# Attention logits of two query blocks at a time: one whole-array pass each, and two half-array passes in two row groups of TensorE

## The chip, the cores and the metric

The kernel runs on one core of one Trainium2 chip. The metric is the device time of one execution in microseconds (us), the median over several runs. Five engines of the core matter here: TensorE (PE in the profile; PEld is its weight loads, which have a row of their own), VectorE (DVE), ScalarE (ACT), GpSimd (POOL), and SyncE (SP), whose queue issues nearly all DMA transfers.

## The reference

The program is one layer of a decoder block: a mixer in which eight heads of forgetting attention stand beside a gated unit with spatial mixing, and then a gated feed-forward part with a short convolution. The sequence has 1024 positions, the model 1024 channels, and all is float32. The part that is changed is the logits of the attention, for each head `h` and each block of 128 queries:

```python
logits = jnp.einsum('bqhd,bkhd->bhqk', qi, k).astype(jnp.float32) * scale   # Dh = 64
logits = logits + ci[..., None] - c_k          # c = cumsum(log_sigmoid(forget))
logits = jnp.where(causal, logits, -jnp.inf)
p = jax.nn.softmax(logits, axis=-1).astype(v.dtype)
return jnp.einsum('bqhk,bkhd->bqhd', p, v)
```

A head has 64 channels, 1024 keys and 8 blocks of queries. Block `j` needs keys 0 to 128(j+1) only.

## The kernel before, in words

**Numbers in two parts.** TensorE is fed float32 values in a rounded format (`F32R`), one pass for each product. To keep float32 precision each operand is split into a high part (rounded) and a low part (what the rounding left), and a product is made of several passes. Elsewhere three passes are made: high by high, high by low, low by high.

**Logits before.** A head has only 64 channels, and a pass contracts over 128 rows of the array. So the high part of the queries is put in rows 0 to 63 and the low part in rows 64 to 127 of one tile `A`. The tile `B` has the keys in the same way (high over low), `B2` has them turned over (low over high). One pass of `A` with `B` gives high by high plus low by low; one with `B2` gives high by low plus low by high. Each logits tile of 128 queries by up to 512 keys (a "piece", `(j, c)`, `c` the first key) is these two passes, at L1007 and L1008, into one of three PSUM banks (`lbank`). There are 12 pieces in a head, 96 in all: in a head, 6 are 512 keys wide, and two each 128, 256 and 384.

**Around it.** `Head` holds a head's tiles; `head_loads` fetches `A`, `B`, `B2` and the row `ck` of forget sums from DRAM scratch (`qd`, `kd`, `ncd`, written by the projection stage before). `select` masks the forget row on GpSimd, `least` (L1015) adds it to the logits on VectorE while it finds the row minimum, `expo` makes the exponentials on ScalarE, `turn` (L1028) transposes them on TensorE, `cast` and `lows` split them, and `weigh` (L1047) multiplies them with the values. `Gated` gives the same loop a filling of other TensorE work: the output projection of the gated unit (`fl`, L1123). A loop of 96 steps runs over heads and groups; before the change each step takes one piece from `stream`, and 10 pieces are made before the loop.

**What sets the order.** Everything up to the end of attention is written down in that loop and then ordered again by a planner in the kernel (`Pace`): `settle` collects the instructions with their dependences and a table of costs (`cost`), `run` simulates the engines and picks for each engine the ready instruction with the earliest due time. The order of each engine, SP's transfers included, is fixed to what it picks. What comes after `settle` (output projection of the attention at L1364 to L1366, then the feed-forward part) is not planned by it.

**Scratch tiles.** Tag `raw` is a ring of four 512 KB tiles for weights as they come from DRAM; during attention it holds the weights of the gated unit's output (`wos`) and then those of the attention's (`woa`, four of them, all loaded at step 54).

Of the kernel before, what the change touches and what calls it, by code (L numbers as in the profile page):

```python
# [14 lines left out]
P = 128  # L15
# [17 lines left out]
class Pace:  # L33
# [1 line left out]


    def __init__(self, tc):
        self.tc, self.slot, self.ring, self.prev, self.held = tc, {}, {}, {}, {}

    def keep(self, t, key):  # L40

# [108 lines left out]
    def settle(self, rounds=3):  # L150

        names = {mybir.EngineType.PE: "PE", mybir.EngineType.DVE: "DVE", mybir.EngineType.Activation: "ACT",
                 mybir.EngineType.Pool: "POOL", mybir.EngineType.SP: "SP"}
        ops, seen, uses, opens = [], {}, {}, {}
        for i in list(self.tc.nc.cur_bb.bb.instructions)[self.first:]:
            eng = names.get(i.engine)
            rd = [v for v in map(self.view, i.ins) if v]
            wr = [v for v in map(self.view, i.outs) if v]
            if eng is None or not wr:
                continue  # L160
            k = len(ops)
            if eng == "PE" and not i.start_tensor_calc:
                rd = rd + wr
            deps = set()
            for w, vs in ((False, rd), (True, wr)):
                for name, a, b, m, tile_ in vs:
                    old, keep, hits = seen.setdefault(name, []), [], 0
                    for o in old:
                        hit = o[2] < b and a < o[3] and o[4] & m
                        if hit and (w or o[1]):  # L170
                            deps.add(o[0])
                            hits += 1
                        if not (w and hit and a <= o[2] and o[3] <= b and not o[4] & ~m and tile_):
                            keep.append(o)
                    keep.append((k, w, a, b, m))
                    seen[name] = keep
                    if tile_:
                        uses.setdefault(name, set()).add(k)
                        if not hits:
                            opens.setdefault(name, set()).add(k)  # L180
            deps.discard(k)
            c = self.cost(i, eng)
            ops.append((i, eng, c, deps, SET.get(str(getattr(i, "func", "")).split(".")[-1], 0) if eng == "ACT" else 0))
        for name, ks in opens.items():
            old = self.prev[name]
# [4 lines left out]
        n = len(ops)  # L190
        succ = [[] for _ in range(n)]
        for k, o in enumerate(ops):
            for d in o[3]:
                succ[d].append(k)
        line, count = [k for k in range(n) if not ops[k][3]], [len(o[3]) for o in ops]
        for k in line:
            for q in succ[k]:
                count[q] -= 1
                if not count[q]:
                    line.append(q)  # L200
        assert len(line) == n, [(ops[k][0].name, str(ops[k][0])) for k in range(n) if count[k]][:4]
        at, t = [0.0] * n, 0.0
        for k, o in enumerate(ops):
            at[k] = t
            if o[1] == "PE":
                t += o[2][0]
        best = None
        for _ in range(rounds):
            due = [0.0] * n
            for k in reversed(line):  # L210
                o = ops[k]
                d = at[k] if o[1] == "PE" else at[k] + SLACK
                for s in succ[k]:
                    d = min(d, due[s] - o[2][1] - HOP)
                due[k] = d
            order, start, end = self.run(ops, succ, due)
            if best is None or end < best[0]:
                best = (end, order)
            at = start
        for eng, seq in best[1].items():  # L220
            for x, y in zip(seq, seq[1:]):
                self.tc.add_manual_dep(ops[y][0], ops[x][0].name, mybir.DependencyInfo(
                    mybir.DependencyClass.NoSync, mybir.DependencyReason.DATA), reason="order")
        return best[0]

    def run(self, ops, succ, due):
# [6 lines left out]
        port = {"DVE": 0.0, "POOL": 0.0}  # L233
        order = {e: [] for e in can}
        start = [0.0] * n
        bus, table, done, end = 0.0, 0, 0, 0.0
        for k in range(n):
            if not left[k]:
                can[ops[k][1]].append(k)
        while done < n:  # L240
            pick = None
            for e, ks in can.items():
# [5 lines left out]
                s = max(f, ready[k])  # L248
                if pick is None or s < pick[0]:
                    pick = (s, k)  # L250
            s, k = pick
            i, e, (cad, lat, x), deps, fn = ops[k]
            can[e].remove(k)
            if fn and fn != table:
# [36 lines left out]
def block_kernel(ctx: ExitStack, tc: tile.TileContext, xT, xtok, wuv, wv, wqk, wf, cpk, bfv,  # L291
# [50 lines left out]
    def f32(ap):  # L342
        return ap.bitcast(F32)
# [466 lines left out]
    def head_loads(h):  # L810
        ab, nb = sb("x1", [P, 2, 1024], F32R), sb("x2", [P, 2, 1024], F32R)
        A, B, ck, B2 = ab[:, 0, :], ab[:, 1, :], f32(nb[:, 0, :]), nb[:, 1, :]
        sp.dma_start(out=f32(A), in_=qd[h].rearrange("s d t -> (s d) t"))
        sp.dma_start(out=f32(B), in_=kd[h].rearrange("s d t -> (s d) t"))
        sp.dma_start(out=f32(B2[0:64, :]), in_=kd[h, 1])
        sp.dma_start(out=f32(B2[64:128, :]), in_=kd[h, 0])
        sp.dma_start(out=ck, in_=ncd[h:h + 1, :].to_broadcast((P, 1024)))
        return A, B, ck, B2

# [156 lines left out]
    attT = [None] * 4  # L976
    attF = [None] * 4
    TTAG = [("gg", "gg"), ("wy", "wy"), ("G0", "G2"), ("G1", "G3")]
    PIECES = [(j, c) for j in range(8) for c in range(0, (j + 1) * P, 512)]
    GROUPS = [(0, k) for k in range(4)] + [(1, k) for k in range(8)]  # L980

    class Head:

        def __init__(self, h):
            self.h, self.p, self.hh = h, h // 2, h % 2
            self.A, self.B, self.ck, self.B2 = loaded.pop(h, None) or head_loads(h)
            self.rs = sml.tile([P, 8], F32, tag="rs", name=nm("rs"))
            self.pair, self.t, self.lg, self.pt, self.po, self.mn = {}, {}, {}, {}, {}, {}

# [11 lines left out]
        def logits(self, j, c):  # L1001

            n = (j + 1) * P
            e = min(n, c + 512)
            qs = slice(j * P, (j + 1) * P)
            ps = self.lg[j, c] = lbank()
            pe.matmul(ps[:, 0:e - c], self.A[:, qs], self.B[:, c:e], start=True, stop=False)  # L1007
            pe.matmul(ps[:, 0:e - c], self.A[:, qs], self.B2[:, c:e], start=False, stop=True)  # L1008

        def least(self, j, c):  # L1010

# [60 lines left out]
    def pair_end(p, eng):  # L1072
# [3 lines left out]
        for o in (slice(0, 512), slice(512, 1024)):  # L1076
# [4 lines left out]
            eng.tensor_tensor(out=attT[p][:, 1, o], in0=f[:, 0, o], in1=f32(attT[p][:, 0, o]), op=ALU.subtract)  # L1081
            yield

    class Gated:


# [3 lines left out]
            self.place = sb("t01", [P, 2, 512])  # L1090

        def load_w(self, hf, kp):
            self.raw[hf, kp] = sb("raw", [P, 2, 512])
            sp.dma_start(out=self.raw[hf, kp], in_=wos[hf, kp])

        def split(self, hf, k):
# [40 lines left out]
    wo, wraw = [], []  # L1137

    def wo_load():
        for k in range(4):  # L1140
            wraw.append(sb("raw", [P, 1024]))
            sp.dma_start(out=wraw[k], in_=woa[k])

    def wo_split(k, hf, lo_eng):
        if hf == 0:
# [5 lines left out]
        w = wo[k][hf]  # L1151
        split_w(wraw[k][:, hf * 512:hf * 512 + 512], (w[:, 0], w[:, 1]), "act", lo_eng)

    STEPS, FILL_RATE = 96, 2.13
    heads = [Head(0)]
    exps, lates, stream = [], [], [(h, j, c) for h in range(8) for j, c in PIECES]
    FIRST = [PIECES[n] for n in (0, 1, 4, 5, 2, 3, 6, 7, 8, 9, 10, 11)]
    stream = [(0, j, c) for j, c in FIRST] + stream[12:]
    picks, nsel = [], [0]
    for h, j, c in stream:  # L1160
        if (h, j) not in picks:
            picks.append((h, j))

    def w1(k):
        return tsplit(wvr[k][:, 1, :])
# [8 lines left out]
    def piece():  # L1174

        if not stream:
            return
        h, j, c = stream.pop(0)
        if (j, c) == (0, 0) and 0 < h < 7:
            heads.append(Head(h + 1))  # L1180
        while nsel[0] < len(picks) and nsel[0] <= picks.index((h, j)) + 1 and picks[nsel[0]][0] < len(heads):
            heads[picks[nsel[0]][0]].select(picks[nsel[0]][1])
            nsel[0] += 1
        heads[h].logits(j, c)
        lates.append((h, j, c))

    def finish_piece():
        for h, j, c in lates:
# [11 lines left out]
    for i in range(8):  # L1200
# [5 lines left out]
        if 1 <= i <= 4:  # L1206
            spatial_out(2 * i - 2)
            spatial_out(2 * i - 1)
            w1s.append(w1(i - 1))
        if i in (0, 2):  # L1210
            evac_v(i, vds[i // 2][:, 0, :])
            evac_v(i + 1, vds[i // 2][:, 1, :])
        if i == 4:
# [1 line left out]
                gated.load_w(0, kp)  # L1215
            gated.load_x((0, 0))
            heads.append(Head(1))
        for _ in range((0, 0, 1, 1, 1, 2, 2, 2)[i]):
            piece()
            finish_piece()  # L1220
        if i >= 4:
# [13 lines left out]
    for s in range(STEPS + BEHIND + 1):  # L1235
# [15 lines left out]
        run_exps()  # L1251
        if s < STEPS:
            heads[h].lows(*GROUPS[g])
        piece()
        finish_piece()
        if g == 2 and h < 8:
            heads[h].sums_a()
        for m in {0: (0, 1, 2), 1: (3,)}.get(s, ()):
# [534 lines left out]
```

## Time and profile before

| | |
|---|---|
| median of 3 runs | 1074.86 us (1074.78 to 1076.51) |
| profiled execution: time / span of the records | 1075.99 us / 1074.3 us |
| TensorE matmul busy | 1053.2 us, 98% of the span, 4885 matmuls |
| weight loads busy | 865.8 us |
| VectorE, ScalarE, GpSimd busy | 905.7, 574.8, 238.9 us |
| first to last logits pass | 208.8 to 364.5 us |

Busy time of TensorE is not the same as work at its peak: matmuls overlap (a pass of 512 columns is shown with 389 ns, while passes in a row start 227 ns apart), so the start-to-start distance is what a pass costs. A DMA's time to landing is counted from its issue. The profile is of one execution.

### The profile page before, as it was taken

The numbers are of one execution on the slowest core, as the hardware profiler recorded it, in microseconds if no ns is written. First come the engines' busy times: TensorE is split into PE (matmuls) and PEld (weight loads), VectorE is DVE, ScalarE is ACT, GpSimd is POOL, SyncE is SP. The second block draws the span as 40 slices with busy tenths as digits, with TensorE's granted clock in tenths as the row PEclk, the third lists the DMA queues.
The fourth block names the chain that finished last, engine by engine and source line by source line (L and its number), as shares of the span: only waits on it lengthen the run. The fifth ranks groups of instructions, "written<-read, shape, count | busy, mean of one in ns | idle before, by whom it ended". The sixth has DMA issues, their size and how long they took to land.

```text
span 1074.3 us, 14284 instructions
## 1 busy us (share of the span) xinstructions
PE 1053.2 (98%) x4885; PEld 865.8 (81%) x4885; DVE 905.7 (84%) x1390; ACT 574.8 (54%) x1006; POOL 238.9 (22%) x211
## 2 busy tenths in 40 slices
PE   9999999999999999998999999999999999999997
PEld 6888778788888877876888888888888888888886
DVE  6986699898888868999899899998998776898774
ACT  6657445577776746753444444444344444454653
POOL 0002224232362250054233232233322000000000
PEclk9999999999999999999999999999999999999999
DMA  9243336886675354223323323232331998333442
GB/s 333 96 145 98 90 115 176 265 255 189 193 220 158 109 199 164 77 73 125 120 67 119 126 82 115 99 114 83 108 118 50 302 342 305 106 92 99 144 122 96
DMA packets 64712, 158.16 MB, mean 147 GB/s; under 512 B 7672, under 2 KB 7936, under 8 KB 64640
## 3 DMA queue, kind: packets, MB, share of 16 engines
q1 hardware_dynamic: 64352, 156.70, 44.8%
q8 instruction: 38, 0.62, 0.2%
q10 hardware_dynamic: 288, 0.56, 0.1%
q14 instruction: 34, 0.28, 0.1%
HBM read 114.95 MB, written 42.27 MB: 146 GB/s over the span
## 4 chain that ended last, share of the span: by engine, by line
PE 82%; issue 7%; DVE 5%; DMA 3%; POOL 2%; ACT 1%; SPq 0%; POOLq 0%; DVEq 0%; ACTq 0%
PE s L1455 20%; PE b L1455 14%; PE s L1650 11%; PE b L1650 8%; PE s L493 6%; PE b L493 5%; PE fl L1123 4%; PE po L1047 3%; PE tr L1028 3%; PE b L635 2%; PE s L635 2%; PE lg L1008 2%; PE lg L1007 2%; DMA qd<-G 1%; DMA x<-kd 1%
## 5 line engine op out<-in xcount | busy, mean ns | idle before, releaser
L1455 PE MATMUL s<-xT,whb 128*128 128x512 f32 x804 | 189.8, 389 | 0.2 <-DVE u L1517 0.2
L1455 PEld LDWEIGHTS s<-xT,whb 128*128 128x128 f32 x804 | 150.7, 188 | 32.0 <-DVE u L1517 0.6
L1455 PE MATMUL b<-xB,wha 128*128 128x512 f32 x528 | 127.2, 390 | 2.0 <-DVE wha L396 2.0
L1650 PE MATMUL s<-whb,wha 128*128 128x512 f32 x528 | 120.2, 389 | 0.0
L1455 PEld LDWEIGHTS b<-xB,wha 128*128 128x128 f32 x528 | 98.9, 188 | 22.8 <-DVE wha L396 2.4
L1650 PEld LDWEIGHTS s<-whb,wha 128*128 128x128 f32 x528 | 99.1, 188 | 20.7
L390 ACT CAST wha<-sg 128x512 fp32r<-128x512 f32 x77 | 48.0, 623 | 97.1 <-PE b L1650 46.0
L390 ACT CAST whb<-sg 128x512 fp32r<-128x512 f32 x82 | 50.6, 618 | 74.8 <-PE s L1455 67.1
L1650 PE MATMUL b<-whb,wha 128*128 128x512 f32 x396 | 90.2, 389 | 0.0
L396 DVE TENSOR_TENSOR wha<-sg,wha 128x512 fp32r<-128x512 f32 x77 | 53.0, 690 | 41.9 <-ACT wha L390 41.9
L1650 PEld LDWEIGHTS b<-whb,wha 128*128 128x128 f32 x396 | 74.3, 188 | 15.4
L1123 PE MATMUL fl<-whl,H 128*128 128x512 f32 x192 | 71.5, 416 | 0.0
L396 DVE TENSOR_TENSOR whb<-sg,whb 128x512 fp32r<-128x512 f32 x82 | 62.8, 767 | 9.0 <-ACT whb L390 8.7
L1455 PE MATMUL s<-xB,whb 128*128 128x512 f32 x264 | 64.9, 395 | 4.6 <-DVE h L1527 4.6
L1455 PEld LDWEIGHTS s<-xB,whb 128*128 128x128 f32 x264 | 50.4, 192 | 15.6 <-DVE h L1527 5.0
L1455 PE MATMUL b<-xT,whb 128*128 128x512 f32 x252 | 61.0, 389 | 0.0
L1342 POOL TENSOR_TENSOR sg<-raw 128x512 f32<-128x512 f32 x20 | 28.1, 1404 | 146.9 <-DVE whb L396 84.0
L1047 PE MATMUL po<-pt,V 128*128 128x512 f32 (+1 forms) x192 | 58.8, 364 | 1.0 <-DVE pt L1039 1.0
L1039 DVE TENSOR_TENSOR pt<-tr,pt 128x512 fp32r<-128x512 f32 (+2 forms) x96 | 51.9, 551 | 8.6 <-ACT pt L1034 8.1
L1034 ACT CAST pt<-tr 128x512 fp32r<-128x512 f32 (+3 forms) x96 | 45.4, 475 | 25.8 <-PE tr L1028 23.1
L1455 PEld LDWEIGHTS b<-xT,whb 128*128 128x128 f32 x252 | 47.2, 188 | 10.0 <-DVE whb L396 0.3
L1343 POOL TENSOR_TENSOR sg<-sg,raw 128x512 f32<-128x512 f32 x20 | 41.2, 2058 | 62.7 <-issue 62.6
(382 smaller groups left out, 2344.1 us busy)
## 6 DMA issues: line engine op xcount, KB each, us to landing
raw<-wup SPq DMA_DIRECT2D x44, 512.0 KB, 3.6
sg<-hx SPq DMA_DIRECT2D x77, 256.0 KB, 2.6
hx<-hs SPq DMA_DIRECT2D x44, 256.0 KB, 2.2
hx<-ca SPq DMA_DIRECT2D x33, 256.0 KB, 2.0
xT<-wdn SPq DMA_DIRECT2D x28, 256.0 KB, 4.8
raw<-wqk SPq DMA_DIRECT2D x8, 512.0 KB, 3.9
qd<-G SPq DMA_DIRECT2D x16, 256.0 KB, 9.3
kd<-G SPq DMA_DIRECT2D x16, 256.0 KB, 3.2
```

Source lines behind the costliest of these rows:

```text
L390: act.copy(h, src)
L396: return eng.tensor_tensor(out=l, in0=src, in1=f32(h), op=ALU.subtract)
L493: pe.matmul(banks[m], xs(n, xi, k)[:, ms], w[:, wi, :], start=(first and k == 0 and c == 0), stop=(k == 3 and c == 2), skip_group_check=True)
L635: pe.matmul(ps, w[:, wi, ks], xs(n, xi, k), start=(first and c == 0), stop=(c == 11), skip_group_check=True)
L1028: pe.transpose(ps[:, (q - 4 * hf) * P:(q - 4 * hf + 1) * P], self.t[q][:, k * P:(k + 1) * P], ident)
L1034: act.copy(pt[:, 0, o:512], ps[:, o:512])
L1039: dve.tensor_tensor(out=pt[:, 1, o:512], in0=ps[:, o:512], in1=f32(pt[:, 0, o:512]), op=ALU.subtract)
L1047: pe.matmul(self.po[hf][:, o:512], lhs, pt[:, s, o:512], start=(k == 0 and s == 0), stop=(k == 4 * hf + 3 and s == 1), skip_group_check=True)
L1123: pe.matmul(self.bank, sgT[k][:, xi, ts_], self.w[hf, k][:, wi, :], start=(k == 0 and i == 0), stop=(k == 3 and i == 2))
L1343: pool.tensor_tensor(out=s[1], in0=s[0], in1=a11, op=ALU.add)
L1455: pe.matmul(ps, w[:, wi, ks], xb[:, xi, k, :], start=(first and n == 0), stop=(n == 11), skip_group_check=True)
L1650: pe.matmul(banks[bk + m], xh[:, xi, ms], wh[:, wi, :], start=(first and p_ == 0 and n == 0), stop=(p_ == NP - 1 and n == 2), skip_group_c ...
```

## The change

For two query blocks `j` and `j+1` the pieces are now made together. `B` holds the high part of the keys in both halves of the rows, `B2` the low part in both halves. The first pass of a piece, `A` with `B` over all 128 rows, gives high by high plus low (queries) by high (keys). What remains is high (queries) by low (keys): 64 rows. These two remaining passes, one for each of the two pieces, use rows 0 to 63 of the array for block `j` and rows 64 to 127 for block `j+1`, next to each other in TensorE's queue. The low by low product is no longer made. For the second one the high part of the odd blocks' queries must lie in partitions 64 to 127, so each head gets one more transfer, `D`, into a new tile `odds`. It takes one place of the `raw` ring (`raw.0`); the three others are given out by name, and the four loads of `woa` are issued at steps 54, 55, 56 and 93. The loop makes a pair of pieces at each odd step, 5 pairs ahead of the loop. In the planner the two half-array passes of a pair are tied (`twin`): the second is placed directly behind the first, the first is entered with a cost of 4 ns and the second with at least 218 ns.

```diff
+    def twin(self, a, b):
+        self.twins[a.ins.name] = b.ins.name
...
+        for a, b in self.twins.items():
+            a, b = place[a], place[b]
+            self.pairs[a] = b
+            ops[a][3].update(ops[b][3] - {a})
+            ops[b][3].add(a)
+            c, d = ops[a][2], ops[b][2]
+            ops[a] = ops[a][:2] + ((4.0, max(c[1], d[1]), 0),) + ops[a][3:]
+            ops[b] = ops[b][:2] + ((max(c[0], d[0], 218.0), max(c[1], d[1]), 0),) + ops[b][3:]
...
-            s, k = pick
+            s, k = pick if then is None else (max(free["PE"], ready[then]), then)
+            then = self.pairs.get(k)
...
-        sp.dma_start(out=f32(B), in_=kd[h].rearrange("s d t -> (s d) t"))
-        sp.dma_start(out=f32(B2[0:64, :]), in_=kd[h, 1])
-        sp.dma_start(out=f32(B2[64:128, :]), in_=kd[h, 0])
+        for r in (slice(0, 64), slice(64, 128)):
+            sp.dma_start(out=f32(B[r, :]), in_=kd[h, 0])
+        for r in (slice(0, 64), slice(64, 128)):
+            sp.dma_start(out=f32(B2[r, :]), in_=kd[h, 1])
...
-    PIECES = [(j, c) for j in range(8) for c in range(0, (j + 1) * P, 512)]
+    PIECES = [((j, c), (j + 1, c)) for j in (0, 2, 4, 6) for c in range(0, (j + 1) * P, 512)]
...
+            self.D = odds[64:128, self.hh, :]
+            sp.dma_start(out=f32(self.D).rearrange("d (m t) -> d m t", t=P),
+                         in_=qd[h, 0].rearrange("d (m o t) -> d m o t", o=2, t=P)[:, :, 1, :])
...
-            pe.matmul(ps[:, 0:e - c], self.A[:, qs], self.B[:, c:e], start=True, stop=False)
-            pe.matmul(ps[:, 0:e - c], self.A[:, qs], self.B2[:, c:e], start=False, stop=True)
+            for j, c in pieces:
+                e, qs = min((j + 1) * P, c + 512), slice(j * P, (j + 1) * P)
+                ps = self.lg[j, c] = lbank()
+                pe.matmul(ps[:, 0:e - c], self.A[:, qs], self.B[:, c:e], start=True, stop=False)
+            for m, (j, c) in enumerate(pieces):
+                e, qs = min((j + 1) * P, c + 512), slice(j * P, (j + 1) * P)
+                r = slice(64 * m, 64 * m + 64)
+                q = self.A[0:64, qs] if m == 0 else self.D[:, j // 2 * P:(j // 2 + 1) * P]
+                two.append(pe.matmul(self.lg[j, c][:, 0:e - c], q, self.B2[r, c:e], start=False, stop=True))
+            pace.twin(*two)
...
-        for _ in range((0, 0, 1, 1, 1, 2, 2, 2)[i]):
+        for _ in range((0, 0, 1, 0, 1, 0, 1, 1)[i]):
...
-        piece()
-        finish_piece()
+        if s % 2 == ODD:
+            piece()
+            finish_piece()
...
-        if s == 54:
+        if s in (54, 55, 56, 93):
             wo_load()
```

TensorE's row before, in the middle of the second head (`lg` are logits banks, `x_217` the tile with `A` and `B`, `x_218` that with `B2`, `fl` the filling work, `tr` transposes; a weight load that goes with each matmul is folded into its row):

```order
L1007 MATMUL lg_2187<-x_217_1831 128x128
L1008 MATMUL lg_2187<-x_218_1832,x_217_1831 128x128
L1123 MATMUL fl_2172<-whl_1952,H_230_1888 128x512 x2
L1007 MATMUL lg_2210<-x_217_1831 128x512
L1008 MATMUL lg_2210<-x_218_1832,x_217_1831 128x512
L1123 MATMUL fl_2172<-whl_1952,H_230_1888 128x512
L1123 MATMUL fl_2172<-whl_1996,H_239_1937 128x512
```

The two passes of a piece stand by themselves, each a whole-array pass, with filling work between the pieces.

TensorE's row now, at the end of the first head (`raw_1715` is the tile `odds`; the first pass is L1026 now, the half-array passes are L1031, the filling work L1150):

```order
L1150 MATMUL fl_2034<-whl_1992,H_238_1937 128x512
L1026 MATMUL lg_2047<-x_170_1551 128x512
L1031 MATMUL lg_2045<-x_171_1552,x_170_1551 128x384
L1031 MATMUL lg_2047<-x_171_1552,raw_1715 128x512
L1150 MATMUL fl_2034<-whl_1992,H_238_1937 128x512
L1026 MATMUL lg_2095<-x_218_1834 128x128
L1150 MATMUL fl_2034<-whl_1992,H_238_1937 128x512
```

All 48 pairs stand like this: two half-array passes next to each other, and a whole-array pass ahead of them and behind them.

SP's row of transfers before, where the tiles of the third head are fetched:

```order
L1142 DMA raw_3240<-woa 128x1024
L1142 DMA raw_3242<-woa 128x1024
L813 DMA x_269_2062<-qd 128x1024
L814 DMA x_269_2062<-kd 128x1024
L815 DMA x_270_2063<-kd 64x1024
L816 DMA x_270_2063<-kd 64x1024
L817 DMA x_270_2063<-ncd 128x1024
```

And now, at the same place:

```order
L1121 DMA raw_2481<-wos 128x1024
L828 DMA x_273_2078<-qd 128x1024
L830 DMA x_273_2078<-kd 64x1024 x2
L832 DMA x_274_2079<-kd 64x1024 x2
L1004 DMA raw_1715<-qd 64x4x128
L833 DMA x_274_2079<-ncd 128x1024
L1169 DMA raw_3247<-woa 128x1024
```

The keys come in four transfers in place of three with the same bytes, `D` (L1004) is added, and the `woa` loads have moved behind the head's tiles.

More of the change, by code (lines that the diff above doesn't have):

```diff
@@ L37, in __init__ @@
     def __init__(self, tc):
-        self.tc, self.slot, self.ring, self.prev, self.held = tc, {}, {}, {}, {}
+        self.tc, self.slot, self.ring, self.prev, self.held, self.twins = tc, {}, {}, {}, {}, {}
+    def twin(self, a, b):
+        self.twins[a.ins.name] = b.ins.name
     def keep(self, t, key):
@@ L190, in settle @@
         n = len(ops)
+        place = {o[0].name: k for k, o in enumerate(ops)}
+        self.pairs = {}
+        for a, b in self.twins.items():
[6 more added lines that the diff above has]
+            ops[b] = ops[b][:2] + ((max(c[0], d[0], 218.0), max(c[1], d[1]), 0),) + ops[b][3:]
         succ = [[] for _ in range(n)]
@@ L235, in run @@
         start = [0.0] * n
-        bus, table, done, end = 0.0, 0, 0, 0.0
+        bus, table, done, end, then = 0.0, 0, 0, 0.0, None
         for k in range(n):
@@ L999, in select, with logits @@
                                compare_op=ALU.is_ge, fill=BIG, base=j * P - c0, channel_multiplier=1)
[L1001 to L1008, printed above, removed]
+        def logits(self, pieces):
+            two = []
+            for j, c in pieces:
[8 more added lines that the diff above has]
+            pace.twin(*two)
         def least(self, j, c):
@@ L1082, in pair_end, with raw @@
             yield
+    def raw(tag, shape, dt=F32):
+        return raws.tile(shape, dt, tag=tag, bufs=1, name=nm("raw"))
     class Gated:
@@ L1092, in load_w @@
         def load_w(self, hf, kp):
-            self.raw[hf, kp] = sb("raw", [P, 2, 512])
+            self.raw[hf, kp] = raw(("raw.1", "raw.2", "raw.3", "raw.1")[hf * 2 + kp], [P, 2, 512])
             sp.dma_start(out=self.raw[hf, kp], in_=wos[hf, kp])
@@ L1139, in wo_load @@
     def wo_load():
-        for k in range(4):
-            wraw.append(sb("raw", [P, 1024]))
-            sp.dma_start(out=wraw[k], in_=woa[k])
+        k = len(wraw)
+        wraw.append(raw(("raw.2", "raw.3", "raw.1", "raw.2")[k], [P, 1024]))
+        sp.dma_start(out=wraw[k], in_=woa[k])
     def wo_split(k, hf, lo_eng):
@@ L1152, in wo_split @@
         split_w(wraw[k][:, hf * 512:hf * 512 + 512], (w[:, 0], w[:, 1]), "act", lo_eng)
+    ODD = 1
     STEPS, FILL_RATE = 96, 2.13
[L1155 to L1162, printed above, removed]
+    heads = []
+    exps, lates = [], []
+    stream = [(h, two) for h in range(8) for two in PIECES]
+    picks, nsel = [(h, j) for h in range(8) for j in range(8)], [0]
     def w1(k):
@@ L1177, in piece @@
             return
-        h, j, c = stream.pop(0)
-        if (j, c) == (0, 0) and 0 < h < 7:
+        h, two = stream.pop(0)
+        if two == PIECES[0] and 0 < h < 7:
             heads.append(Head(h + 1))
-        while nsel[0] < len(picks) and nsel[0] <= picks.index((h, j)) + 1 and picks[nsel[0]][0] < len(heads):
+        while nsel[0] < len(picks) and nsel[0] <= picks.index((h, two[1][0])) + 1 and picks[nsel[0]][0] < len(heads):
             heads[picks[nsel[0]][0]].select(picks[nsel[0]][1])
             nsel[0] += 1
-        heads[h].logits(j, c)
-        lates.append((h, j, c))
+        heads[h].logits(two)
+        lates.extend((h, j, c) for j, c in two)
     def finish_piece():
@@ L1209, in block_kernel @@
             w1s.append(w1(i - 1))
+        if i == 1:
+            odds = raw("raw.0", [P, 2, 512], F32R)
+            heads.append(Head(0))
         if i in (0, 2):
```

## The prediction

> **What bounds the kernel now.** I read the page's head first, then the chain of work that ended last, then the busy time by stage over the part where logits are made.
>
> ```profile
> PE 1053.2 (98%) x4885; PEld 865.8 (81%) x4885; DVE 905.7 (84%) x1390; ACT 574.8 (54%) x1006; POOL 238.9 (22%) x211
> ...
> PE 82%; issue 7%; DVE 5%; DMA 3%; POOL 2%; ACT 1%; SPq 0%; POOLq 0%; DVEq 0%; ACTq 0%
> ...
> core 0: us, PE busy (x) PEld busy (x) DVE busy (x) ACT busy (x) POOL busy (x), PEclk, DMA share, GB/s
> 208.00:232.00 24.00, 24.00 (x127) 20.00 (x126) 21.38 (x44) 16.08 (x33) 9.61 (x15) 1.00 0.96 304
> 232.00:364.60 132.60, 132.59 (x786) 111.81 (x785) 111.38 (x296) 97.85 (x229) 47.30 (x73) 1.00 0.59 177
> 364.60:400.00 35.40, 34.39 (x171) 28.22 (x170) 25.78 (x42) 18.79 (x38) 14.90 (x11) 1.00 0.52 176
> ```
>
> TensorE makes 82% of the chain. In the two stretches that hold all logits (208 to 364.6) it is never idle and its clock is full, while VectorE has 21.2 of 132.6 us free in the long one and ScalarE 34.8. So what a logits piece costs TensorE from one pass's start to the next one's lies on the path one for one, both ways, and VectorE only comes into it if the stage shrinks by some 21 us.
>
> **What a pass costs today.** The instructions of the first heads in order of time; the columns are start, length, engine, line, operation:
>
> ```profile
> 234.56 0.39 PE L1007 MATMUL lg<-x 128*128 128x512 f32 x1
> 234.79 0.40 PE L1008 MATMUL lg<-x,x 128*128 128x512 f32 x1
> 235.02 0.22 PE L1007 MATMUL lg<-x 128*128 128x128 f32 x1
> 235.08 0.27 PE L1008 MATMUL lg<-x,x 128*128 128x128 f32 x1
> 235.19 0.90 PE L1123 MATMUL fl<-whl,H 128*128 128x512 f32 x3
> ...
> 236.04 0.28 PE L1008 MATMUL lg<-x,x 128*128 128x256 f32 x1
> 236.16 0.40 PE L1123 MATMUL fl<-whl,H 128*128 128x512 f32 x1
> ...
> 238.11 0.34 PE L1008 MATMUL lg<-x,x 128*128 128x384 f32 x1
> 238.28 0.27 PE L1028 MATMUL tr<-ident,wy 128*128 128x128 f32 x1
> ```
>
> From a second pass's start to the next start: 0.23 us at 512 columns, 0.17 at 384, 0.12 at 256, 0.11 at 128. The lengths (0.39) overlap and are no price.
>
> **The first passes** stay as many and as wide, so they cost nothing more or less. Their operand `B` has other contents only.
>
> **The second passes** become pairs. Each head has six: two of 512 with 512 columns, two of 384 with 512, two of 128 with 256. Today a pair costs 0.46, 0.40 and 0.23 us; the 48 pairs together 8 x 2 x 1.09 = 17.4 us. What a pair costs side by side depends on what it takes to go from the whole array to half of its rows and back, since every pair has whole-array passes ahead and behind. The profile has one such place, far from the logits: the sums of the forget gate (L729) contract over 64 rows, between whole-array passes of L635 (the last column of a row in brackets is the engine's idle time ahead of it and what ended it; x16 is sixteen instructions in a row):
>
> ```profile
> 117.79 0.40 PE L635 MATMUL b<-H,whl 128*128 128x512 f32 x1
> ...
> 118.11 0.18 PEld L729 LDWEIGHTS s<-gg,whl 64*128 64x128 f32 x1 [0.36 <-issue]
> ...
> 118.11 1.86 PEld L729 LDWEIGHTS s<-gg,whl 64*128 64x128 f32 x16 [0.36 <-issue]
> ...
> 119.67 0.30 PEld L729 LDWEIGHTS s<-gg,whl 64*128 64x128 f32 x2
> ...
> 119.99 0.30 PEld L635 LDWEIGHTS b<-H,whl 128*128 128x128 f32 x2
> ...
> 117.07 1.27 ACT L720 COPY whl<-s 64x512 f32<-64x512 f32 x2 [2.47 <-PE s L718]
> ```
>
> Going in: the last whole-array pass starts at 117.79. Its successor would normally start at 118.02 with its weights loaded meanwhile. Here the first 64-row load starts only at 118.11, 0.32 after, and waits for nothing the profile shows: the first of ScalarE's two copies, which it needs, was over by 117.7. The 16 loads then come (1.86 - 0.19) / 15 = 0.11 apart, so a load takes 0.11 and the first 64-row pass can stream at 0.43 in place of 0.23: **entry 0.20**. Going out: the last of the 64-row loads starts at 119.67 + 0.30 - 0.19 = 119.78, its pass of 8 columns streams from 119.89; the whole-array load behind it starts at 119.99 and the next 0.11 later, so the whole-array pass streams at 120.10: **exit 0.21** behind a pass that takes next to nothing itself. In both, about 0.10 is emptying the array and 0.11 a load that is not hidden. L729 also differs in its number format (plain float32, where the logits have the rounded one); that the wait comes from the rows and not from the format is my reading.
>
> Does every change of shape do this? Passes of 64 output columns (L718) alternate with full ones:
>
> ```profile
> 112.85 0.39 PE L635 MATMUL b<-x,wy 128*128 128x512 f32 x1
> 113.08 0.40 PE L718 MATMUL s<-x,whl 128*64 128x512 f32 x1
> 113.31 0.39 PE L718 MATMUL s<-t,whl 128*64 128x512 f32 x1
> 113.55 0.39 PE L635 MATMUL b<-x,wy 128*128 128x512 f32 x1
> ```
>
> No: 0.23 apart, as without a change. Narrower columns are free, fewer rows were not. The Trainium skill (TensorEngine Tiling (Array Packing), Tiling Modes, Key Properties) says that changing the tiling mode drains TensorE, for rows and columns alike; by it these rows of L718 should show a gap, which they don't, so the trace bears it out for rows alone. It gives no time for the drain.
>
> **A pair side by side**, then: entry 0.20; the second row group's weights another 0.11, in which the first group already streams; the wider pass w (0.23 or 0.12); exit 0.21. That is 0.52 + w: 0.75 for 512 with 512 and for 384 with 512, 0.64 for 128 with 256. Against today +0.29, +0.35, +0.41. A head: 2 x 1.05 = 2.10; eight heads **+16.8 us**. Bounds: nothing for entry and exit at all gives the first rival below; both as here and the two groups not at the same time adds 0.12, 0.06 and 0 per pair, 2.9 us in all.
>
> **The order of pieces and the banks.** Pairs come every other step, so VectorE gets two tiles at a time. Its reductions of logits, shortest, median and longest in ns, and below that what it waited for, in us and times:
>
> ```profile
> L1015 DVE CUSTOM_DVE_ANT_0 G<-lg,x,lim x32: 732/750/753, 217.7 to 364.0; 128x512 f32<-128x512 f32 x32
> ...
>   PE lg L1008: 12.8, 27
> ```
>
> A reduction takes 0.75 us at most, two 1.5, and a pair comes every (364.5 - 208.8) / 48 = 3.2 us; so a bank is free again long before the ring of three returns to it. VectorE waits 12.8 us for logits today and has room for that in the 21 us. I cost it at nothing; if that cover went, the next one late would be the exponentials and transposes of the step, at most 0.75 per pair in the pairs where it happens.
>
> **Transfers.** `B` in two transfers in place of one is 8 more issues, and `D` 8 more of 128 KB. The head's transfers today:
>
> ```profile
> 224.80 10.09 SPq L1142 DMA_DIRECT2D raw<-woa  x2
> 235.22 0.33 SPq L813 DMA_DIRECT2D x<-qd  x1
> 235.59 0.42 SPq L814 DMA_DIRECT2D x<-kd  x1
> 236.11 0.49 SPq L815 DMA_DIRECT2D x<-kd  x1
> ...
> x<-qd SPq DMA_DIRECT2D x8, 512.0 KB, 5.7
> ```
>
> An issue takes 0.3 to 0.5 us of a queue that stands still 10 us waiting for `raw` tiles; 16 more issues in 156 us are 8 us of the queue, one microsecond a head, ordered a head ahead. In the long stretch DMA is busy to 0.59, and `D` is a quarter of one of a head's 512 KB loads. Nothing on the path. `woa` now stands behind the third head's tiles, which come sooner. The place without cover is the change of stages:
>
> ```profile
> 203.91 0.82 PE L493 MATMUL s<-whl,x 128*128 128x512 f32 x2 [1.87 <-DVE G L887]
> ```
>
> TensorE waits 1.87 us behind a tile that VectorE frees only when slow writes have landed. Head 0's tiles are in that traffic with nearly the same transfers in another order: I take 0, with -2 to +2. The last `woa` tile is loaded once the first one's splits are over:
>
> ```profile
> 367.24 1.13 ACT L390 CAST whl<-raw 128x512 fp32r<-128x512 f32 x2
> ...
> raw<-woa SPq DMA_DIRECT2D x4, 512.0 KB, 4.1
> ...
> 393.75 0.39 PE L1364 MATMUL b<-G,G 128*128 128x512 f32 x1
> ```
>
> Those casts end at 368.4, the load takes 4.1, its split some 3 us; its products start at 393.75 (the first pass of the fourth of the four parts). That leaves 18 us, and the 72 passes of the other three parts are the cover. Nothing. After attention nothing is changed, and its start moves with TensorE.
>
> **Sum.** 1075.99 (the profiled execution: span 1074.3 and 1.7 around it) + 16.8 = 1092.8. The median of the runs is 1.13 below that execution, so the forecast against it is **1091.7 us**, 1.6% slower.
>
> **Rivals.**
> *The switch is free* (faster). The wait at L729 would be due to its number format, and row groups would come and go as the 64 columns of L718 do. Then a pair costs the wider pass, but not less than two loads, 0.22: 0.23, 0.23, 0.22 in place of 0.46, 0.40, 0.23. A head saves 2 x 0.41, eight 6.6 us: 1068.3. VectorE's 21 us of room bear that. For it speak L718 and the unexplained format; against it that both waits fit an array being emptied, on the way in and out. It decides the sign once entry, stagger and exit together stay under 6.6 / 48 = 0.14 us a pair, against the 0.52 taken above. The Trainium skill (TensorE: Matmul & The Clock Gate, Part 3: Packing small matmuls, Measured speedup vs the span model) gives about 4 ns between the starts of passes in different row groups, which would be this case; no run here shows it.
> *Emptied, but the loads are hidden.* Entry 0.32 - 0.23 = 0.09, exit 0.10, no stagger: 0.19 + w is 0.42, 0.42 and 0.31 (0.41 if both loads have to fit in). Per head 2 x (-0.04 + 0.02 + 0.08 or 0.18): 1.0 to 2.6 us slower, 1075.9 to 1077.5. Against it: the load at 118.11 did wait, with 0.36 us of idle time ahead of it.
> *Not side by side*: the groups take turns, as bounded above: 1094.6. Nothing in this profile shows two groups at once.
>
> **How the numbers follow.** A difference under 0.2%, 2.1 us, is about what a measurement of this kernel cannot tell from none. The forecast has 0.62, the free switch 0.23, the hidden loads 0.10, the turns 0.05. Slower: 0.62 + 0.05 + 0.03 of the hidden loads = 0.70; within 0.2%: 0.07; faster 0.23. The likeliest case by itself: one of its loads hidden in each pair takes off 5.3, the change of stages 2 either way, the turns add 2.9, so 1084.4 to 1096.6. Both signs have too much to be left out, so the range goes down to the free switch, 1067.5 to 1096.5; what is left out is some 0.1 at the two ends.
>
> **What the profile after would show.** If I am right, in front of the first weight load of each pair some 0.3 us from the last whole-array start, and the whole-array pass behind it starting about 0.4 after the second half-array pass's stream should have ended; the count of matmuls stays, the stretch from the first to the last logits pass grows by about 17 us, and VectorE waits longer for logits. If the switch is free, the two passes start some ns or 0.11 apart and the next whole-array pass 0.23 later. Wrong in another way I would be if the 1.87 us at 203.91 became many, or if transposes waited for exponentials.

## The result, and the profile after

The changed kernel takes **1089.1 us** (median; 1087.4 to 1092.6) against 1075.7 for the kernel before beside it: a ratio of 1.0129, interval 1.0101 to 1.0156. It is 13.4 us slower; the forecast was 1091.7. Two later comparisons of the same kernel on other occasions gave 1.0119 (1.0104 to 1.0134) and 1.0126 (1.0111 to 1.0141).

The head of the page and the engines in the chain that ended last, of the profiled execution (1092.6 us, the longest of the four, span 1090.9):

```profile
PE 1065.0 (98%) x4885; PEld 862.5 (79%) x4885; DVE 903.3 (83%) x1390; ACT 573.9 (53%) x1006; POOL 238.5 (22%) x211
...
PE 84%; issue 6%; DVE 4%; DMA 3%; POOL 1%; ACT 1%; SPq 0%; POOLq 0%; DVEq 0%; ACTq 0%
```

The count of matmuls is the same, TensorE is still the bound, and VectorE has the same work. By stage, with the columns as in the prediction:

```profile
208.00:232.00 24.00, 23.66 (x107) 18.23 (x107) 20.07 (x43) 13.22 (x26) 6.73 (x11) 0.93 1.00 308
232.00:377.00 145.00, 145.00 (x808) 110.74 (x807) 115.27 (x301) 101.31 (x236) 49.11 (x78) 1.00 0.59 167
```

In the long stretch TensorE is never idle and its clock is full, as before. But it needs 145 us for 808 matmuls where it took 132.6 for 786, 0.179 for one in place of 0.169: some matmuls cost more. The half-array passes, by line (duration in ns: least, median, longest), and what their weight loads waited for, in us and times:

```profile
L1031 PEld LDWEIGHTS lg<-x,x x48: 182/183/183, 216.4 to 377.4; 64*128 64x128 f32 x48
L1031 PE MATMUL lg<-x,raw x48: 379/492/502, 217.0 to 377.5; 64*128 64x512 f32 x32, 64*128 64x256 f32 x16
  issue: 8.9, 34
```

Ahead of 34 loads the row of weight loads stood idle, 8.9 us in all, and waited for nothing that the profile shows. One pair in order of time, the matmuls:

```profile
237.85 0.40 PE L1026 MATMUL lg<-x 128*128 128x512 f32 x1
238.18 0.49 PE L1031 MATMUL lg<-x,x 64*128 64x512 f32 x1
238.18 0.49 PE L1031 MATMUL lg<-x,raw 64*128 64x512 f32 x1
238.60 0.44 PE L1052 MATMUL tr<-ident,gg 128*128 128x128 f32 x2
```

and the weight loads, with the idle time ahead of each:

```profile
238.18 0.18 PEld L1031 LDWEIGHTS lg<-x,x 64*128 64x128 f32 x1 [0.37 <-issue]
238.18 0.18 PEld L1031 LDWEIGHTS lg<-x,raw 64*128 64x128 f32 x1
238.60 0.20 PEld L1052 LDWEIGHTS tr<-ident,gg 128*128 128x128 f32 x2 [0.24 <-issue]
```

Read it so: the last whole-array pass starts at 237.85, and the first half-array load 0.33 us later, not meanwhile. The two loads start together (3 to 4 ns apart in the records), and so do the two passes. The next whole-array load starts 0.42 after them, and it has to end (0.11) before its pass can stream. From 237.85 to 238.71 is 0.86; the whole-array pass itself is 0.23 of that, so **the pair costs 0.63** where two whole-array passes cost 0.46. A pair of 128 and 256 columns:

```profile
320.54 0.34 PE L1026 MATMUL lg<-x 128*128 128x256 f32 x2
320.81 0.33 PE L1031 MATMUL lg<-x,x 64*128 64x128 f32 x1
320.81 0.38 PE L1031 MATMUL lg<-x,raw 64*128 64x256 f32 x1
321.12 0.30 PEld L1071 LDWEIGHTS po<-pt,V 128*128 128x128 f32 x2
```

Here the next load comes 0.31 after the pair. With an entry as above the pair is 0.33 + 0.31 + 0.11 - 0.23 = 0.52, against 0.23. So by rows the three kinds of pair cost 0.17, 0.23 and 0.29 more than whole-array passes, and 8 x 2 x 0.69 = 11.0 us in all. Some cost less: in this example the last pass ahead is a narrow one. It ends at 320.88, and at the 0.22 that a pass of 128 columns has in the prediction's rows it begins 0.15 before the load, so part of the emptying lies in the 0.11 that such a pass takes anyway.

What the pairs cost in sum is seen best on the filling work, 192 matmuls spread over the attention loop, whose first and last start frame it. Before and after:

```profile
L1123 PE MATMUL fl<-whl,H x192: 387/397/482, 231.8 to 368.9; 128*128 128x512 f32 x192
```

```profile
L1150 PE MATMUL fl<-whl,H x192: 387/397/506, 236.7 to 382.3; 128*128 128x512 f32 x192
```

The loop went from 137.1 to 145.6 us. It holds 44 of the 48 pairs (four stand ahead of the first filling), so 0.19 a pair and **9.2 us for all 48**. The 145.6 repeats to 0.1 us in three profiles of the changed kernel. The same frame for all kernels that were run (the edits are described below; "ahead" is the first start of the filling, "behind" the span less its last start; each from one profile):

| kernel | span | ahead | loop | behind |
|---|---|---|---|---|
| before | 1074.3 | 231.8 | 137.1 | 705.4 |
| whole-array passes, surroundings of after | 1072.3 | 230.7 | 137.0 | 704.6 |
| the same again | 1076.5 | 234.0 | 137.1 | 705.4 |
| the same, keys fetched as in after | 1075.8 | 231.6 | 137.1 | 707.1 |
| after | 1090.9 | 236.7 | 145.6 | 708.6 |
| after, second | 1085.5 | 234.5 | 145.6 | 705.4 |
| after, third | 1088.1 | 235.2 | 145.6 | 707.3 |
| after, first head without `D` | 1083.8 | 234.5 | 145.6 | 703.7 |
| same rows | 1092.6 | 235.0 | 152.9 | 704.7 |
| four banks | 1086.7 | 235.8 | 146.1 | 704.8 |
| fours | 1080.8 | 233.7 | 141.9 | 705.2 |
| singles | 1110.3 | 236.9 | 169.2 | 704.2 |

The loop is steady; the two other columns scatter by up to 3.3 us between executions of one and the same kernel. Part of that is TensorE's granted clock: from 200 to 212 us, around its wait for VectorE, its mean was 1.00 in the first profile of the whole-array kernel and 0.72 in the second, and that alone is up to 3.4 us (12 x 0.28).

### The profile page after: what moved, and what is told of

It reads as the page before. It is cut to its first block, busy times and chain, and to the rows that moved or that the text cites. A ratio compares the mean times of both kernels' runs of the same rounds, so it can differ in the third digit from the quotient of the medians.

```text
span 1090.9 us, 14302 instructions
## 1 busy us (share of the span) xinstructions
PE 1065.0 (98%) x4885; PEld 862.5 (79%) x4885; DVE 903.3 (83%) x1390; ACT 573.9 (53%) x1006; POOL 238.5 (22%) x211
## 4 chain that ended last, share of the span: by engine, by line
PE 84%; issue 6%; DVE 4%; DMA 3%; POOL 1%; ACT 1%; SPq 0%; POOLq 0%; DVEq 0%; ACTq 0%
PE s L1483 20%; PE b L1483 15%; PE s L1678 10%; PE b L1678 8%; PE s L508 5%; PE b L508 5%; PE fl L1150 4%; PE po L1071 3%; PE tr L1052 3%; PE b L650 2%; PE s L650 2%; PE lg L1031 2%; PE lg L1026 2%; DMA qd<-G 1%; DMA x<-kd 1%
## 5 line engine op out<-in xcount | busy, mean ns | idle before, releaser
L1150 PE MATMUL fl<-whl,H 128*128 128x512 f32 x192 | 69.1, 430 | 0.0
L1058 ACT CAST pt<-tr 128x512 fp32r<-128x512 f32 (+2 forms) x96 | 45.6, 476 | 38.5 <-PE tr L1052 32.6
```

What stands on the lines that cost most here:

```text
L1058: act.copy(pt[:, 0, o:512], ps[:, o:512])
L1150: pe.matmul(self.bank, sgT[k][:, xi, ts_], self.w[hf, k][:, wi, :], start=(k == 0 and i == 0), stop=(k == 3 and i == 2))
```

## The experiments

**Is it the half-array passes, or what stands around them?** The changed kernel with its order, banks, transfers and planner ties, but whole-array second passes; `B` and `B2` have their parts as before the change again:

```diff
-                two.append(pe.matmul(self.lg[j, c][:, 0:e - c], q, self.B2[r, c:e], start=False, stop=True))
+                two.append(pe.matmul(self.lg[j, c][:, 0:e - c], self.A[:, qs], self.B2[:, c:e], start=False, stop=True))
```

> The changed kernel with the second passes of a pair made over the whole array (operands as before the change: high over low against low over high); the order on TensorE, VectorE, ScalarE and GpSimd, the extra transfer, the tile odds and the pairs stay. Theory of the switch (0.41 us for each way into the row groups and back, on top of the wider pass): a pair falls from 0.64, 0.64, 0.53 us to 0.46, 0.40, 0.23, so 8 x 2 x 0.72 = 11.5 us off 1089.1: 1077.6 us, between 1076 and 1079.5; what is left above 1075.7 is the price of the new order and transfers. Rival, the surroundings (two tiles at a time for VectorE, one more transfer, three raw tiles): no difference, 1089 us.

Measured: 1076.2 against 1076.0, ratio 1.0004 (0.9993 to 1.0015). The long stretch of this kernel:

```profile
232.00:365.00 133.00, 133.00 (x789) 113.49 (x788) 111.00 (x296) 97.63 (x230) 48.12 (x73) 1.00 0.66 187
```

789 matmuls in 133 us, as before. The new order of pieces, the pairs that come to VectorE at once, the 16 further transfers and the planner's numbers cost nothing that can be measured. What this kernel leaves out, beside the half-array passes, is a wait for `D`: the transfer is there, but no pass reads it. The slowdown belongs to the half-array passes and, at most, to that wait.

**Are the two passes really side by side?** Both in rows 0 to 63 (`D` placed in partitions 0 to 63), everything else in the order of after:

```diff
-            self.D = odds[64:128, self.hh, :]
+            self.D = odds[0:64, self.hh, :]
...
-                r = slice(64 * m, 64 * m + 64)
+                r = slice(0, 64)
```

> The changed kernel with both half-array passes of a pair in rows 0 to 63, one after the other; the order of all engines is the same. Theory that the two row groups do run side by side: the first pass of a pair now has its own time again, 0.23, 0.17 and 0.11 us in the three kinds of pair, 8 x 2 x 0.51 = 8.2 us more: 1097.3 us, 1095 to 1099.5. Rival, they already take turns (the profile only shows their starts 4 ns apart): 1089 us.

Measured: 1094.8 against 1076.0, 1.0179 (1.0160 to 1.0199). One pair, its loads:

```profile
309.11 0.18 PEld L1034 LDWEIGHTS lg<-x,x 64*128 64x128 f32 x1 [0.36 <-issue]
309.22 0.19 PEld L1034 LDWEIGHTS lg<-x,raw 64*128 64x128 f32 x1
309.77 0.30 PEld L1154 LDWEIGHTS fl<-whl,H 128*128 128x128 f32 x2 [0.37 <-issue]
```

and its passes:

```profile
309.11 0.50 PE L1034 MATMUL lg<-x,x 64*128 64x512 f32 x1
309.45 0.39 PE L1034 MATMUL lg<-x,raw 64*128 64x512 f32 x1
```

The second load comes 0.11 after the first, the next whole-array load 0.66 after it where it was 0.42 with two row groups. So the 0.23 of one pass is what lying side by side saves, as asked of it. The loop is 7.3 us longer than after, 8.0 for 48 pairs, close to the 8.2 expected; the whole time, 1094.8, came out just under the range of 1095 to 1099.5. In after the passes do run at once, and it is the way in and out that eats the gain.

**What does one half-array pass by itself cost?** The kernel before, in its own order, with every second pass on rows 0 to 63 alone and no pairs. Like the changed kernel, it leaves out low by low, and it fetches the keys as that one does:

```diff
-            pe.matmul(ps[:, 0:e - c], self.A[:, qs], self.B2[:, c:e], start=False, stop=True)
+            pe.matmul(ps[:, 0:e - c], self.A[0:64, qs], self.B2[0:64, c:e], start=False, stop=True)
```

> The kernel before with one edit: the second pass of each piece is made over rows 0 to 63 alone (high queries by low keys; the product low by low is left out, as in the changed kernel). No pairs, no extra transfer, four raw tiles, one piece a step. Theory of the switch: 95 ways there and back of 0.41 us, 39 us more than 1075.7: 1114.6 us, 1109 to 1119. Rival, the surroundings of the change: nothing of them is here, so 1075.7 us.

Measured: 1112.4 against 1076.0, 1.0339 (1.0322 to 1.0355).

```profile
309.60 0.18 PEld L1009 LDWEIGHTS lg<-x,x 64*128 64x128 f32 x1 [0.24 <-issue]
310.02 0.19 PEld L1124 LDWEIGHTS fl<-whl,H 128*128 128x128 f32 x1 [0.24 <-issue]
```

0.42 from the half-array load to the next whole-array load: one pass alone costs what a pair does. The kernel makes 95 visits to the half array and loses 36.4 us, 0.38 for each. TensorE's passes come in the order of the kernel before, and there is no `D`, so neither a new order nor `D` is needed for the loss.

**Does the cost go by the visit or by the pass?** Four half-array passes (two pairs) in a row, 24 visits in place of 48. That needs a fourth logits bank, so first a control, pairs with the banks that the fours use:

```diff
-        return ring_bank("lg", (0, 1, 2))
+        return ring_bank("lg", (0, 1, 2, 3))
...
-        return ring_bank("tr", (3, SP_[2]))
+        return ring_bank("tr", (SP_[2], SP_[1]))
...
-        return ring_bank("fl", (SP_[0], SP_[1]))
+        return ring_bank("fl", (SP_[0],))
```

> The control for fours: the changed kernel with four banks for logits in place of three, one for the filling work in place of two (the last values leave theirs before the loop). Pairs and 48 ways there and back as before. Both theories: as the changed kernel, 1089 us, 1087 to 1093 if the single filling bank makes some waits.

Measured: 1086.5 against 1075.0, 1.0097 (1.0080 to 1.0114); the loop 146.1. Somewhat faster than expected, but not in the loop, where the banks are. Then the fours:

```diff
+    FOURS = [PIECES[n] + PIECES[n + 1] for n in (0, 2, 4)]
-    stream = [(h, two) for h in range(8) for two in PIECES]
+    stream = [(h, two) for h in range(8) for two in FOURS]
...
-        if s % 2 == ODD:
+        if s % 4 == ODD:
```

> The same banks, and two pairs in one visit to the row groups: four first passes, then four half-array passes in a row. The same passes, 24 ways there and back in place of 48. Theory of the switch: 24 x 0.41 = 9.8 us less than the control, about 1079.3, 1077 to 1082, which is still some 2 us above before. Rival, a half-array pass is slow in itself (cost by pass, not by visit): as the control, 1089.

Measured: 1079.4, 1.0042 (1.0028 to 1.0057), 7.1 less than the control, where 9.8 less was expected. One visit:

```profile
235.00 0.40 PE L1030 MATMUL lg<-x 128*128 128x512 f32 x1
235.33 0.18 PEld L1036 LDWEIGHTS lg<-x,x 64*128 64x128 f32 x1 [0.36 <-issue]
235.33 0.18 PEld L1036 LDWEIGHTS lg<-x,raw 64*128 64x128 f32 x1
235.43 0.19 PEld L1036 LDWEIGHTS lg<-x,x 64*128 64x128 f32 x1
235.44 0.19 PEld L1036 LDWEIGHTS lg<-x,raw 64*128 64x128 f32 x1
235.99 0.20 PEld L1059 LDWEIGHTS tr<-ident,gg 128*128 128x128 f32 x2 [0.37 <-DVE V L931]
```

0.33 in, and 0.66 to the next whole-array load: a second pair adds 0.66 - 0.42 = 0.24, one pass of 512 columns. Its loads come 0.11 behind the first ones, while those passes stream. So the cost does go by the visit. In the loop the gain is smaller than in the whole time: 146.1 to 141.9, 4.2 us where 22 visits fewer of 0.41 make 9.0; the other 2.9 us of the 7.1 lie outside the loop, where equal kernels scatter as much. Much of what the loop lacks went to waits. Weight loads in the stretch from 208 to 383, in us, times and longest, in the control and in the fours:

```profile
PEld tr L1052 <- DVE pt L1063: 0.6, 3, 0.2
```

```profile
PEld tr L1059 <- DVE pt L1070: 2.7, 9, 0.8
PEld po L1078 <- DVE t L1087: 0.8, 2, 0.4
```

Four tiles at once now make TensorE wait for VectorE's results, some 3 us in all. What pairs did not do, fours do. Of the other 2 us that the loop lacks, 1.1 go if a visit is put at the 0.36 that the loop of after gives (0.19, and the 0.17 that a pair saves on average); the rest was not traced to a cause.

**Is the rest of the loss the late `D` of the first head?** The changed kernel was run again, beside the fours:

> The changed kernel again, for a narrower interval beside the runs of the same chip: 1089 us, 13 us above before. By its profile the 48 ways there and back cost 0.41 us each over the wider pass, 11.5 us in sum, so a median of 1087.5 would be the least that this accounts for.

It measured 1088.4, 1.0119 (1.0104 to 1.0134). Its profile shows a wait that the forecast did not have, a pass of the first pair:

```profile
214.78 0.38 PE L1031 MATMUL lg<-x,raw 64*128 64x256 f32 x1 [2.37 <-DMA raw<-qd]
```

SP's queue ahead of it:

```profile
206.48 0.33 SPq L828 DMA_DIRECT2D x<-qd  x1
206.86 1.12 SPq L830 DMA_DIRECT2D x<-kd  x2
208.08 1.20 SPq L1004 DMA_DIRECT2D raw<-qd  x2
```

`D` is issued behind the second head's `A` and `B`, and its pass waits 2.4 us for it (0.3 and 0.4 in the two other profiles). To take the wait away, the first head's odd blocks use rows 64 to 127 of `A`, which are there; this makes that head's second product another one (low by low in place of high by low), with the same passes:

```diff
-                q = self.A[0:64, qs] if m == 0 else self.D[:, j // 2 * P:(j // 2 + 1) * P]
+                q = self.A[r, qs] if m == 0 or self.h == 0 else self.D[:, j // 2 * P:(j // 2 + 1) * P]
```

> The changed kernel in which the first head's odd blocks take their half-array operand from the tile A (its low part, so that for this head this product is another one) and not from the extra transfer D; the transfer stays, the order of all engines is the same. In the profile of the changed kernel taken again the first pair waits 2.37 us for D of the first head. If that wait is on the path: 1088.4 - 2.4 = 1086.0, and the 11.5 us of the 48 visits are then all that is left above 1075.0. If other work at the change of stages is as late: 1088.4, no difference.

> The changed kernel beside it, on the same chip: 1088.4 us, 1087 to 1090.

Measured: 1087.7 (1.0121, 1.0104 to 1.0137) beside 1088.7 for after (1.0126, 1.0111 to 1.0141). One microsecond apart, within both intervals: inconclusive by the times. The filling starts at 234.5 us in the kernel without the wait, and at 234.5 also in the profile that waited 2.4. But these two profiles cannot be set side by side as they are: from 200 to 212 us the mean granted clock was 0.72 in the first and 1.00 in the second, which is worth up to 3.4 us to the second. TensorE's idle time up to the filling, in which the clock counts little, is 6.7 us without the wait and 9.2 with it. So the traces speak for a wait that lies on the path when it is long, and the times do not decide it.

**Is it the keys, fetched from the same addresses twice?** `B` takes the high part of the keys twice now, and `B2` the low part. The whole-array kernel with the keys fetched like that, `B2` likewise (its products are others then):

```diff
-        for m, r in enumerate((slice(0, 64), slice(64, 128))):
-            sp.dma_start(out=f32(B[r, :]), in_=kd[h, m])
+        for r in (slice(0, 64), slice(64, 128)):
+            sp.dma_start(out=f32(B[r, :]), in_=kd[h, 0])
```

> The kernel with whole-array second passes (e1), but its keys fetched as the changed kernel fetches them: each half of B from the high part, each half of B2 from the low part, so that its products are others; the order of all engines is that of e1. In the profiles so far TensorE's wait near 202 us for a slow write of the queries is 2.8 to 4.6 us where one part of the keys is read twice in a row, and 1.9 and 2.2 us where it isn't. If the repeated read makes it: 3.3 us here, and 1 to 2 us more than e1, 1077.5. If not: about 2 us, and 1076.2.

> One more profile of e1 beside it: if the wait near 202 us goes with the repeated read, about 2 us; if it varies by itself, anything from 1.9 to 4.6.

Measured: 1076.1 against 1074.9, 1.0010 (0.9999 to 1.0021), and 1078.2 in the one run of the whole-array kernel beside it. What was asked about is the wait for VectorE's tile behind the slow writes, in after and in these two:

```profile
PE s L508 <- DVE G L903: 3.5, 1, 3.5
```

```profile
PE s L511 <- DVE G L906: 2.5, 1, 2.5
```

```profile
PE s L511 <- DVE G L906: 3.1, 1, 3.1
```

It is 1.9 to 3.1 us in the four profiles of kernels with whole-array passes, and 2.8 to 4.6 in those with half-array ones. The way of fetching does not explain it: the kernel without it waited longer than the one with it. Nor can the half-array passes: the wait is over by 208 us, the first of them starts at 211 us or later, and up to there this kernel and after run the same instructions in the same order on every engine. What sets these profiles apart stays open.

## Why the prediction came out as it did

The direction, the place and the cause were right, and the time lay within the range. But that the figure was close is luck in part, because two errors offset each other: the pairs cost 9.2 us in place of 16.8, and some 4 us came from stretches that were costed at nothing.

**Whether there is a price for the way in and out: right.** The forecast read it off a far place with another number format. At the logits the same 0.33 us from a 512-column pass to the first 64-row load appears with the rounded format, so the format is not its cause. The free switch and the hidden loads fell on this row: the idle 0.37 ahead of the load. Taking turns fell on the same-rows kernel, in which the two passes do take turns and which is slower by 0.5%.

**"The second row group's weights another 0.11": wrong.** This is the term that failed. Loads into two row groups start 3 to 4 ns apart, and the passes too; 0.11 is what two loads into the same rows take, as in the same-rows kernel. The place it was read from had loads into one row group only. So a pair is 0.63 or 0.52 and not 0.75 or 0.64, which takes 48 x 0.11 = 5.3 us off the sum and gives 11.5 (11.0 with the rounded rows above). The Trainium skill (TensorE: Matmul & The Clock Gate, Part 3: Packing small matmuls, Measured speedup vs the span model) gives about 4 ns for each further tile. This case's trace agrees, with 3 to 4 ns between the two groups. The forecast gave that figure to the rival alone in which the switch is free as well; here the two groups start together and the switch has its price.

**Entry 0.20 and exit 0.21 at every pair: a little too much.** The loop shows 9.2 in place of 11.0 for all pairs. Since the whole-array kernel has the same passes in the same order, the two traces can be set side by side, from the pass ahead of a pair to the third pass behind it. Where passes of more than 128 columns stand on both sides (7 of the 44 pairs), the three kinds of pair cost 0.28, 0.21 and 0.18 more, as the rows have it. Where a transpose of 128 columns stands behind, the widest kind costs 0.11 in place of 0.18 (the 5 pairs with wide passes ahead). The pair at 238.18 is one of these: its first transpose can stream at 238.71 and the next starts at 238.77, 0.06 later, while transposes otherwise start 0.11 apart, so half of the load behind the pair is won back. A narrow pass ahead takes off about as much in the smallest kind, 0.23 in place of 0.28 (7 pairs); the example at 320.81 is one of them.

**Order of pieces, banks, transfers in the loop, `woa`, planner at nothing: right.** The whole-array kernel has all of these, but for a wait for `D`, and costs 1.0004. VectorE was forecast to wait longer for logits; it waits about as long:

```profile
DVE wy L1039 <- PE lg L1031: 4.9, 6, 1.1
DVE G L1039 <- PE lg L1031: 4.7, 12, 0.9
DVE gg L1039 <- PE lg L1031: 2.5, 2, 1.4
```

That is 12.1 us, against 12.8.

**Change of stages at 0, within 2: not settled.** By the table, after starts its filling at 235.5 (mean of three), the four kernels with whole-array passes at 232.0; four pairs ahead of the loop account for 0.8. So 2.7 us are left there, and 1.5 behind the loop (707.1 against 705.6); with the 9.2 that is the 13.4 measured. In the traces the 2.7 are idle time of TensorE ahead of its first filling, 8.9 us in the mean of after against 6.2. About 1.0 is the longer wait for VectorE's tile (3.4 against 2.4 in the mean of the same profiles), 0.7 a wait for ScalarE's first tile near 6 us, and 1.0 the wait for `D` (0.3, 2.4 and 0.4). The first two come ahead of all logits passes, where after and the whole-array kernel in its order run the same instructions, so of the three only the wait for `D` can be laid to the half-array passes. Both columns scatter by as much as 2.7 among equal kernels. Yet the three comparisons of after with the kernel before all give 13.4 to 14.0 us, and the pairs and `D` make 10.2 of them; what the rest is remains open.

**Forecast signs in the profile.** The 0.3 ahead of a pair is there behind passes of 512 columns; behind the narrower ones that most pairs follow it is 0.15 to 0.26. The whole-array pass behind a pair was to start 0.4 after the end of the pair's stream; it is 0.19 (0.42 + 0.11 - 0.11 - 0.23), which fits the exit of 0.21 in the sum and not that sentence. The count of matmuls stayed. From the first logits pass to the last it was 155.7 us and is 168.0: 12 more, where 17 were forecast.

## What to carry to other kernels

Two passes on half the rows do run at once here, but a visit to the half array among whole-array passes cost 0.36 (by the loop) to 0.40 us (by the rows) beside the passes themselves (read here as 0.10 on either side to empty the array and two loads of 0.11 that nothing covers), so count visits and not passes. A pair of 512-column passes saves 0.23 and cannot pay for that; a visit must save more than some 0.4, and even four passes in a row stayed 0.4% slower. In this kernel the six pairs of a head take 1.16 us side by side where the whole-array passes take 2.18, so 2.5 to 2.8 visits a head would break even, while three is what four banks allow and they brought waits of their own.

## What was not expected of the hardware

A single 64-row pass among whole-array ones took as long as a pair: 0.42 us from its load to the next whole-array load in both. Loads into different row groups started 3 to 4 ns apart, those into the same rows 0.11. And a second pair behind the first had its loads hidden, while the first pair's were not. That reads as if a load could not begin while passes on another number of rows were still in the array; no run here took that apart further.
